# Encoder block with expert retrieval: output products start after 104 of 128 activation blocks instead of 124

## The chip, the cores and the metric

One core of one Trainium2 chip. The metric is the device time of one execution in microseconds (us), median of three runs; less is better.

## The reference

One layer on 512 tokens of width 1024: a mixer (gated convolution and a linear recurrence), then a retrieval over 16384 single-neuron experts, then a norm. The change is in the retrieval:

```python
q = (xb @ w_q).reshape(p, PEER_HEADS, 2, PEER_DK_HALF)
sc = jnp.einsum('phcd,hcnd->phcn', q, sub_keys).astype(jnp.float32)
top_s, top_i = lax.top_k(sc, PEER_TOPK)          # 16 of 128 keys, twice per head
...                                              # 16 of the 256 pairs: best_s, idx
g = jax.nn.softmax(best_s, axis=-1)
act = jax.nn.gelu(jnp.einsum('phkd,pd->phk', expert_u[idx], xb), approximate=False)
coef = (g * act.astype(jnp.float32)).astype(xb.dtype)
return jnp.einsum('phk,phkd->pd', coef, expert_v[idx])   # p = tokens, h = 8, k = 16
```

Each token uses 128 experts (8 heads by 16). All numbers are float32.

## The kernel before

**Two ways to the same sum.** For 384 tokens (three tiles of 128) the kernel is dense: it multiplies them with all 16384 experts, in 128 blocks of 128 experts, and weights the result with a gate matrix that is zero but at the chosen experts. For the other 128 tokens it is sparse: it gathers the 128 chosen rows of `expert_u` and `expert_v` per token. 64 of the dense tokens take their first product (with `expert_u`) from the sparse way too, so a dense activation block is 128 experts by 320 tokens.

**Jobs.** The dense work is a list of 256 jobs, one block of weights (512 KB) each. A u job loads a block of `uT`, multiplies it with the tokens (24 matmuls of 320 columns, `u_chunk`) and puts GELU of the result in an `act` tile, two blocks to a tile. A v job multiplies block n's gated activations with its block of `expert_v` into six accumulators (18 matmuls of 512 columns, L1037). Float32 weights are split into a high part `whi` (ScalarE, ACT, L78) and a low part `wlo` (VectorE, DVE, L83), and each product is three matmuls. Weights are loaded five jobs ahead (`w_load(k + 5)`), `whi` is made three ahead, `wlo` two ahead.

**Order.** `CE` u jobs come first, then v jobs and the remaining u jobs alternate, then v jobs alone. With CE = 124 that is u0 to u123, four pairs (v, u), then v4 to v127; the last three v jobs are done in a tail. The `act` ring holds 32 blocks (RB). Older blocks go to memory: one store of two blocks (`Ad<-act`, L845), one reload before use (`act<-Ad`, L911). v jobs run in the order `vorder`, which begins at block `v0`; blocks from v0 on need no store.

**What else runs in the u part.** DVE also does the top-16 searches, the gate steps and the dots of the sparse way. A gate step builds one-hot matrices for eight tokens (L627, L632; ACT L643), PE multiplies them, ACT copies the result into `stg` (L667, two buffers), and SP stores it to `Gd` (L678; the last store stands on ACT's queue). The last 16 gate steps (four tokens each, in f32: L617, L620, matmuls L655) wait until the dots of the 64 tokens are done. At u job KD = CE - 6 every gate step must be done; at job CE - 5 the first gates are read back (`gt<-Gd`, L898). A planner `turn()` hands out DVE's time: after each job it emits searches, gate steps or dots until DVE's planned time catches up with PE's, at most two dots a job, no dot in the last QU = 6 jobs before CE, and dots only up to DR times the jobs since they began.

**Sparse steps.** One dot is a gather of 128 rows by GpSimd (POOL, `rows<-in_u_dram`, L767, 512 KB) and one DVE instruction (`scr`, L788) with its accumulator read. There are 64 + 128 dots, then 128 sums (`ys`, L804, rows of `expert_v`). Whatever the u part left over is emitted in the v part: after v job n until the count reaches `share`, rising linearly from v3 on, less 0.31 per job once blocks are reloaded.

**Gates in the v part.** v job n takes its gates from a tile that was read from `Gd`: 16 blocks at a time, in three loads of 1024 KB (L885), alternately into the memory of `h2` (free once the last u job is done) and into `gt`; the first 16 blocks come as two times eight (three loads of 512 KB each, L898). `v_gated` makes `cf` (ACT L918, DVE L920) and `ch` (ACT L924), `v_rest` makes `cl` (DVE L931), for two blocks at a time.

All of this is recorded with a manual schedule: within an engine, and within each DMA queue (SP's, POOL's), instructions run in the order in which they are emitted.

Of the kernel before, what the change touches and what calls it, by code (L numbers as in the profile page):

```python
# [8 lines left out]
F32 = mybir.dt.float32  # L9
# [12 lines left out]
NE = 128  # L22
# [12 lines left out]
def block_kernel(ctx, tc, xT, small, w_ada1, w_ada, b_ada, w_in, w_r, w_i, w_out, w_q, keys, uT, u, v, final_g, out):  # L35
# [4 lines left out]
    persist = ctx.enter_context(tc.tile_pool(name="persist", bufs=1))  # L40
# [27 lines left out]
    h2 = persist.tile([128, 2, KB, T], FR, name="h2")  # L68
# [434 lines left out]
    NG = (T - 128) // 16  # L503
# [309 lines left out]
    ld = lambda k: h2l[:, k, T - NU:]  # L813
    jobs = [("u", c) for c in range(CE)]
    for n in range(NE):
        jobs.append(("v", n))
        if CE + n < NE:
            jobs.append(("u", CE + n))
    wraw, whi, wlo = {}, {}, {}
    v0 = max(CE - RB + 3, 0) // 8 * 8 + 8  # L820
    vorder = list(range(v0, NE)) + list(range(v0))

    def w_load(k):
        if k < len(jobs):
            kind, i = jobs[k]
            wraw[k] = load_w(uT[i] if kind == "u" else
                             v[vorder[i] * 128:(vorder[i] + 1) * 128, :].rearrange("p (k e) -> p k e", k=KB))

    def w_high(k):
        if k < len(jobs):  # L830
            whi[k] = high(wraw[k])

    def w_low(k):
        if k < len(jobs):
            wlo[k] = low(wraw.pop(k), whi[k])
# [14 lines left out]
    def u_evict():  # L850
        if unread:
            c, ps = unread.pop()
            if c % 2 == 0:
                act[c // 2] = ring.tile([128, 2, NU], F32, name="act", bufs=RB // 2)
            nc.scalar.activation(act[c // 2][:, c % 2], ps, AF.Gelu)  # L855

    def u_chunk(k, pool):
        c = jobs[k][1]
        ps = pool.tile([128, NU], F32, name="ps_act", bufs=2)
        mm3(ps, whi.pop(k), wlo.pop(k), hd, ld, range(KB), True, True)  # L860
        u_evict()
        unread.append((c, ps))
        q = c // 2 - RB // 2 + 2
        if c % 2 == 0 and 0 <= q < v0 // 2:
            spill(q)
        pe[0] += 3530
        dve[0] += 1140
        ac[0] += 1400

    gbuf, g16, gdone = {}, {}, set()  # L870
    coef = {}

    def load_g16(m, t):
        if m not in g16:
            if m % 32:
                big = g16[16] if m > 16 else persist.tile([128, 32, 16, 16], F32, name="h2")[:, 0:NG]
            else:
                big = gt8.rearrange("p s g i t -> p (s g i t)").rearrange("p (g i t) -> p g i t", i=16, t=16)
            g16[m] = big
            for k in range(0, 16, 2):  # L880
                gbuf[m + k] = big[:, :, k:k + 2, :]
        for k in range(0, 16, 8):
            cc = vorder[m + k]
            if k == 0 and vorder[m + 8] == cc + 8:
                nc.sync.dma_start(g16[m][:, 8 * t - 8:8 * t], Gd[t][:, :, cc:cc + 16, :].rearrange("g j i t -> j g i t"))  # L885
                return
            nc.sync.dma_start(g16[m][:, 8 * t - 8:8 * t, k:k + 8],
                              Gd[t][:, :, cc:cc + 8, :].rearrange("g j i t -> j g i t"))

    def v_gates(n):  # L890
        if n >= NE or n in gdone:
            return
        gdone.add(n)
        cc = vorder[n]
        if n < 16 and n % 8 == 0:
            gt = gt8[:, n // 8]
            for t in (2, 3, 1):
                nc.sync.dma_start(gt[:, 8 * t - 8:8 * t], Gd[t][:, :, cc:cc + 8, :].rearrange("g j i t -> j g i t"))  # L898
            for k in range(0, 8, 2):
                gbuf[n + k] = gt[:, :, k:k + 2, :]  # L900
        for t in range(1, NT):
            m = n + (4 - t if n < 16 else 13 - 3 * t)
            if m >= 16 and m % 16 == 0 and m < NE:
                load_g16(m, t)

    def v_act(q):
        if q < NE // 2:
            c = vorder[2 * q] // 2
            if act[c] is None:
                act[c] = ring.tile([128, 2, NU], F32, name="act", bufs=RB // 2)  # L910
                nc.sync.dma_start(act[c].rearrange("p c t -> p (c t)"), Ad[c])  # L911

    def v_gated(q):
        if q < NE // 2:
            cf = vp.tile([128, 2, ND], F32, name="cf", bufs=1)
            g = gbuf.pop(2 * q)
            nb = XB // 16
            nc.scalar.activation(cf[:, :, 0:XB].rearrange("p c (g t) -> p c g t", t=16),  # L918
                                 g[:, 0:nb].rearrange("p g c t -> p c g t"), AF.Copy)
            nc.vector.tensor_mul(cf[:, :, XB:].rearrange("p c (g t) -> p c g t", t=16),  # L920
                                 act.pop(vorder[2 * q] // 2).rearrange("p c (g t) -> p c g t", t=16),
                                 g[:, nb:].rearrange("p g c t -> p c g t"))
            ch = vp.tile([128, 2, ND], FR, name="ch", bufs=2)
            nc.scalar.activation(ch, cf, AF.Copy)  # L924
            coef[q] = (cf, ch)

    def v_rest(q):
        if q < NE // 2:
            cf, ch = coef[q]
            cl = vp.tile([128, 2, ND], FR, name="cl", bufs=2)  # L930
            nc.vector.tensor_sub(cl, cf, ch.bitcast(F32))  # L931
            coef[q] = (ch, cl)
# [6 lines left out]
    given = {"s": 0, "r": 0, "g": 0, "d": 0}  # L939
    KD = CE - XE - 1  # L940
    first = []

    def turn(k):

        awake = [g for g in "gsrd" if g in gens and asleep[g] <= k]
        if "d" in awake and (given["d"] >= DR * (k + 1 - first[0]) or k >= CE - QU or xd > k % 2):
            awake.remove("d")
# [22 lines left out]
    for k in range(CE):  # L970
# [12 lines left out]
        while dve[0] < RHO * pe[0] or k == KD:  # L983
# [7 lines left out]
            n = next(gens[g], 0)  # L991
# [13 lines left out]
        if k == KD:  # L1005
# [4 lines left out]
            gt8 = vp.tile([128, 2, NG, 8, 16], F32, name="gt", bufs=1)  # L1010
        m = k - CE + XE
        if 0 <= m < XE:
            for n in [0] if m < 2 else range(5) if m == XE - 1 else [8]:
                v_gates(n)
# [17 lines left out]
    def v_chunk(n, b):  # L1032
        hi, lo, ch, cl = vsp[n]
        bs = slice(b * 128, (b + 1) * 128)
        for st, mv, first, last in ((ch, hi, n == 0, False), (ch, lo, False, False), (cl, hi, False, n == NE - 1)):
            for e in range(2):
                nc.tensor.matmul(accs[b][e], st[:, bs], mv[:, e * 512:(e + 1) * 512], start=first, stop=last)  # L1037
# [12 lines left out]
        nc.vector.tensor_add(frow[0], frow[0], frow[1])  # L1050

    sparse = chain(dot_gen, sum_gen)
    steps, done = len(usteps) - len(bdone) + 128, 0
    for k in range(CE, len(jobs)):
        w_load(k + 5)
        w_high(k + 3)
        w_low(k + 2)
        kind, n = jobs[k]
        if kind == "u":
            u_chunk(k, psP)  # L1060
        else:
            q, e = divmod(n, 2)
            v_gates(n + 5)
            if e == 0:
                v_act(q + 4)
                v_gated(q + 1)
            else:
                v_rest(q + 1)
            vsp[n] = [w.pop(k).rearrange("p k e -> p (k e)") for w in (whi, wlo)] + [c[:, e] for c in coef[q]]
            if n < NE - VT:  # L1070
                for b in range(3):
                    v_chunk(n, b)
                del vsp[n]
            u_evict()
            pe[0] += 4090
            dve[0] += 2005
        if kind == "v":
            share = min(max(n + 1 - QV, 0) / (NE - VE - QV), 1) * (steps + 0.31 * (NE - RB)) - 0.31 * max(n + 1 - RB, 0)
            while done < share and next(sparse, None):
                done += 1  # L1080
    fin = vp.tile([128, 2, 3, D], F32, name="gt", bufs=1)
# [47 lines left out]
VE = 1  # L1129
# [2 lines left out]
NS = 56000  # L1132
DS = 1.0
XD = 2
CE = 124
GB_E = 5
DR = 1.1
QU = 6
QV = 3
RB = 32  # L1140
# [54 lines left out]
```

## Time and profile before

| | us |
|---|---|
| median of 3 runs (1408.8 to 1412.49) | 1411.27 |
| profiled execution, time | 1413.22 |
| its span, first to last instruction | 1411.5 |
| u part, before the first v job (309.30 to 832.15) | 522.85 |
| v0 to the start of the tail (832.15 to 1378.72) | 546.57 |
| tail (1378.72 to the end) | 32.78 |

PE (matmuls) is busy 95% of the span, DVE 87%, ACT 49%, POOL 38%. In the rows that the prediction shows, PEclk is the granted clock of PE as a share of full speed, and the DMA share is the mean busy share of 16 DMA engines. Overlapping packets take it a little over 1. A window's row gives busy time and number of instructions of each engine in turn.

### The profile page before, as it was taken

To read this page: it belongs to the slowest core of one execution; us is meant where nothing else is said; L and a number is where in the kernel's file an instruction comes from. 1 tells how busy PE (TensorE), PEld (TensorE's weight loads), DVE (VectorE), ACT (ScalarE), POOL (GpSimd) and SP (SyncE) were. 2 spreads that over 40 slices of the span, in tenths; PEclk is the share of its full clock that TensorE was granted. 3 is DMA by queue.
4 is the path that set the end of the run, shared out by engine and by line. 5 is a ranking of instruction groups with operands and counts; after the bars stand their busy time and mean duration, and the time that the engine had idled before them with its cause. 6 is when DMAs were issued, how large, how long until landed. Compare 5 with 4: busy or idle time off the path is not lost.

```text
span 1411.5 us, 21746 instructions
## 1 busy us (share of the span) xinstructions
PE 1336.9 (95%) x7739; PEld 1144.7 (81%) x7739; DVE 1222.1 (87%) x2332; ACT 687.6 (49%) x1178; POOL 538.0 (38%) x334
## 2 busy tenths in 40 slices
PE   5999998999998999999999999899989999999995
PEld 2666787779998999998989998777778888878884
DVE  6766555899998999999989847799989889898998
ACT  4544433545377697797744444233333434343442
POOL 0000000000233145344545404576666667576760
PEclk9999999999999999999999999999999999999998
DMA  9675322124678899999999997999999999999994
GB/s 378 225 265 181 124 90 97 61 83 134 203 253 300 290 344 397 357 355 355 417 382 388 403 314 244 411 378 410 403 415 411 404 404 416 412 405 410 406 382 165
DMA packets 146929, 440.07 MB, mean 312 GB/s; under 512 B 14722, under 2 KB 42370, under 8 KB 144772
## 3 DMA queue, kind: packets, MB, share of 16 engines
q1 hardware_dynamic: 99812, 267.75, 51.5%
q0 software_dynamic: 46720, 169.89, 30.8%
q8 instruction: 60, 0.98, 0.3%
q10 hardware_dynamic: 288, 1.05, 0.2%
q14 instruction: 49, 0.40, 0.1%
HBM read 393.54 MB, written 45.09 MB: 311 GB/s over the span
## 4 chain that ended last, share of the span: by engine, by line
DVE 27%; PE 23%; DMA 16%; issue 13%; ACT 4%; DVEq 0%; SPq 0%; ACTq 0%
DMA wraw<-in_v_dram 13%; DVE wlo L83 5%; PE ps_act L92 5%; PE ps_act L94 5%; PE ps_act L93 5%; PE acc L1037 5%; DVE scr L788 4%; DVE ys L804 4%; DMA Gd<-stg 2%; DVE cf L920 2%; DVE cl L931 2%; DVE oh L627 2%; ACT whi L78 1%; DVE rep L457 1%; PE ps_gt L658 1%
## 5 line engine op out<-in xcount | busy, mean ns | idle before, releaser
L78 ACT ACTIVATE whi<-wraw 128x1024 fp32r<-128x1024 f32 x292 | 308.7, 1057 | 404.1 <-DMA wraw<-in_v_dram 157.7
L83 DVE TENSOR_TENSOR wlo<-wraw,whi 128x1024 fp32r<-128x1024 f32 x292 | 356.1, 1220 | 112.5 <-ACT whi L78 111.3
L92 PE MATMUL ps_act<-h,whi 128*128 128x320 f32 x1024 | 322.5, 315 | 8.1 <-ACT act L855 6.9
L94 PE MATMUL ps_act<-h,wlo 128*128 128x320 f32 x1024 | 317.1, 310 | 0.6 <-DVE wlo L83 0.6
L93 PE MATMUL ps_act<-h,whi 128*128 128x320 f32 x1024 | 317.1, 310 | 0.0
L767 POOL DMA_INDIRECT rows<-in_u_dram,idx_s x128 | 201.3, 1573 | 189.0 <-DVE scr L788 162.4
L767 POOL DMA_INDIRECT rows<-in_v_dram,idx_s x128 | 222.7, 1740 | 108.7 <-DVE ys L804 84.9
L1037 PE MATMUL acc<-whi,ch 128*128 128x512 f32 x750 | 233.7, 393 | 9.5 <-ACT ch L924 9.2
L1037 PE MATMUL acc<-whi,cl 128*128 128x512 f32 x750 | 234.6, 394 | 6.1 <-DVE cl L931 6.1
L1037 PE MATMUL acc<-wlo,ch 128*128 128x512 f32 x750 | 233.6, 393 | 0.0
L767 POOL DMA_INDIRECT rows<-in_u_dram,idx_b x64 | 108.9, 1701 | 255.7 <-DVE scr L788 171.8
L92 PEld LDWEIGHTS ps_act<-h,whi 128*128 128x128 f32 x1024 | 193.2, 189 | 10.8 <-ACT act L855 8.7
L94 PEld LDWEIGHTS ps_act<-h,wlo 128*128 128x128 f32 x1024 | 192.9, 188 | 0.9 <-DVE wlo L83 0.9
L93 PEld LDWEIGHTS ps_act<-h,whi 128*128 128x128 f32 x1024 | 193.3, 189 | 0.2
L1037 PEld LDWEIGHTS acc<-whi,ch 128*128 128x128 f32 x750 | 141.6, 189 | 40.7 <-ACT ch L924 10.9
L1037 PEld LDWEIGHTS acc<-whi,cl 128*128 128x128 f32 x750 | 141.6, 190 | 40.1 <-DVE cl L931 11.1
L1037 PEld LDWEIGHTS acc<-wlo,ch 128*128 128x128 f32 x750 | 142.1, 189 | 29.9
L804 DVE SCALAR_TENSOR_TENSOR ys<-rows,acts,ys 128x1024 f32<-128x1024 f32 x127 | 162.6, 1281 | 1.7
L788 DVE SCALAR_TENSOR_TENSOR scr<-rows,h2n 128x1024 f16<-128x1024 f32 x128 | 156.2, 1220 | 2.3 <-DMA rows<-in_u_dram,idx_s 0.6
L643 ACT ACTIVATE igh<-oh,gl 128x128 f16<-128x128 f16 x320 | 104.0, 432 | 47.8 <-DVE oh L627 47.6
L408 POOL DMA_DIRECT2D x1d<-xn x8 | 4.6, 569 | 281.7 <-DVE wlo L83 234.6
L92 PE MATMUL ps_z<-h,whi 128*128 128x512 f32 x224 | 90.8, 409 | 3.2 <-ACT h L216 2.9
(260 smaller groups left out, 1691.2 us busy)
## 6 DMA issues: line engine op xcount, KB each, us to landing
wraw<-in_uT_dram SPq DMA_DIRECT2D x128, 512.0 KB, 6.8
wraw<-in_v_dram SPq DMA_DIRECT2D x128, 512.0 KB, 9.3
Gd<-stg SPq DMA_DIRECT2D x46, 512.0 KB, 9.2
wada<-in_w_ada_dram SPq DMA_DIRECT2D x16, 1024.0 KB, 5.1
Ad<-act SPq DMA_DIRECT2D x48, 320.0 KB, 7.1
act<-Ad SPq DMA_DIRECT2D x48, 320.0 KB, 12.2
h<-Gd SPq DMA_DIRECT2D x12, 1024.0 KB, 18.3
wraw<-in_w_in_dram SPq DMA_DIRECT2D x20, 512.0 KB, 6.1
```

What stands on the lines that cost most here:

```text
L78: nc.scalar.activation(hi, raw, AF.Copy)
L83: nc.vector.tensor_sub(lo, raw, hi.bitcast(F32))
L92: nc.tensor.matmul(ps, hi[:, k, :], xh(k), start=first and k == ks[0], stop=False)
L93: nc.tensor.matmul(ps, hi[:, k, :], xl(k), start=False, stop=False)
L94: nc.tensor.matmul(ps, lo[:, k, :], xh(k), start=False, stop=last and k == ks[-1])
L627: nc.vector.tensor_tensor(flat.rearrange("p (q n b) -> p q n b", q=8, b=2), io2[:, None, :, :].to_broadcast(shp), sij[:, a0].rearrange("p ...
L643: nc.scalar.activation(ig[:, 1, k // 2, :, k % 2], of[:, k // 2, 0, :, k % 2], AF.Copy, scale=gl[:, t0 + k:t0 + k + 1])
L767: nc.gpsimd.indirect_dma_start(out=r[:, :], out_offset=None, in_=table, in_offset=bass.IndirectOffsetOnAxis(ap=idxs[:, k:k + 1], axis=0))
L788: nc.vector.scalar_tensor_tensor(scr, rows.pop(n), 1.0, hn, op0=OP.mult, op1=OP.mult, accum_out=dst[:, k:k + 1])
L804: nc.vector.scalar_tensor_tensor(ys, rows.pop(k), acts[:, k:k + 1], ys, op0=OP.mult, op1=OP.add)
L920: nc.vector.tensor_mul(cf[:, :, XB:].rearrange("p c (g t) -> p c g t", t=16), act.pop(vorder[2 * q] // 2).rearrange("p c (g t) -> p c g t" ...
L1037: nc.tensor.matmul(accs[b][e], st[:, bs], mv[:, e * 512:(e + 1) * 512], start=first, stop=last)
```

## The change

```diff
     def load_g16(m, t):
         if m not in g16:
-            if m % 32:
-                big = g16[16] if m > 16 else persist.tile([128, 32, 16, 16], F32, name="h2")[:, 0:NG]
+            if m % 32 == 0:
+                big = g16[32] if m > 32 else persist.tile([128, 32, 16, 16], F32, name="h2")[:, 0:NG]
...
     def v_gates(n):
...
-        if n < 16 and n % 8 == 0:
-            gt = gt8[:, n // 8]
+        if n < 32 and n % 8 == 0:
+            gt = gt8[:, n // 8 % 2]
...
-            m = n + (4 - t if n < 16 else 13 - 3 * t)
-            if m >= 16 and m % 16 == 0 and m < NE:
+            m = n + (4 - t if n < 32 else 13 - 3 * t)
+            if m >= 32 and m % 16 == 0 and m < NE:
                 load_g16(m, t)
...
+    room = [MX if n < NE - CE else 1.62 if n < 32 else 1.5 for n in range(NE)]
...
-            share = min(max(n + 1 - QV, 0) / (NE - VE - QV), 1) * (steps + 0.31 * (NE - RB)) - 0.31 * max(n + 1 - RB, 0)
+            share = steps * sum(room[QV:n + 1]) / sum(room[QV:NE - VE])
...
-CE = 124
+CE = 104
+MX = 3.4
-DR = 1.1
+DR = 0.9
```

In the program it builds: u0 to u103, 24 pairs (v0, u104) to (v23, u127), then v24 to v127. `v0` moves from block 96 to block 80, so 40 act tiles are stored and reloaded instead of 48. The gates of the first 32 blocks come eight at a time, and the 16-block loads begin with block 32 of the order. The first v job finds 72 dots done instead of 112. The number of dots, sums, gate steps and matmuls is the same.

DVE between early v jobs (numbers behind the names tell the buffers apart). Before, at v6 and v7, with no u job between them:

```order
L83 TENSOR_TENSOR wlo_9701<-wraw_9594,whi_9665 128x1024
L920 TENSOR_TENSOR cf_9703<-act_8590,gt_9187 128x2x320
L788 SCALAR_TENSOR_TENSOR scr_9728,acts_2625<-rows_9659,h2n_1878 128x1024
L788 SCALAR_TENSOR_TENSOR scr_9732,acts_2625<-rows_9689,h2n_1878 128x1024
L83 TENSOR_TENSOR wlo_9738<-wraw_9625,whi_9699 128x1024
L931 TENSOR_TENSOR cl_9740<-cf_9703,ch_9706 128x768
L788 SCALAR_TENSOR_TENSOR scr_9762,acts_2625<-rows_9693,h2n_1878 128x1024
L788 SCALAR_TENSOR_TENSOR scr_9766,acts_2625<-rows_9726,h2n_1878 128x1024
```

After, at u111, v8 and the start of u112 (a `wlo` is for the job two further on):

```order
L83 TENSOR_TENSOR wlo_9092<-wraw_8967,whi_9042 128x1024
L83 TENSOR_TENSOR wlo_9123<-wraw_9009,whi_9090 128x1024
L920 TENSOR_TENSOR cf_9125<-act_7949,gt_8367 128x2x320
L788 SCALAR_TENSOR_TENSOR scr_9151,acts_2625<-rows_9072,h2n_1878 128x1024
L788 SCALAR_TENSOR_TENSOR scr_9155,acts_2625<-rows2_9076,h2n_1878 128x1024
L788 SCALAR_TENSOR_TENSOR scr_9159,acts_2625<-rows_9080,h2n_1878 128x1024
L788 SCALAR_TENSOR_TENSOR scr_9163,acts_2625<-rows_9082,h2n_1878 128x1024
L83 TENSOR_TENSOR wlo_9169<-wraw_9040,whi_9121 128x1024
```

Where each v job had two dots, a pair of jobs now has four (three in every fourth pair), all behind the v job's `wlo`.

DVE at the last gate steps, `selB` being the selected keys of the 64 tokens. Before, at u102 and the start of u103:

```order
L83 TENSOR_TENSOR wlo_8412<-wraw_8276,whi_8408 128x1024
L788 SCALAR_TENSOR_TENSOR scr_8443,acts_2625<-rows_8348,h2n_1878 128x1024
L617 TENSOR_TENSOR oh8_8445<-iota_76,selB_2624 128x512
L620 TENSOR_SCALAR oh8_8445<-iota_76,selB_2624 128x128 x4
L617 TENSOR_TENSOR oh8_8457<-iota_76,selB_2624 128x512
L620 TENSOR_SCALAR oh8_8457<-iota_76,selB_2624 128x128 x4
L83 TENSOR_TENSOR wlo_8473<-wraw_8317,whi_8469 128x1024
L788 SCALAR_TENSOR_TENSOR scr_8504,acts_2625<-rows_8400,h2n_1878 128x1024
```

After, at u91 and the start of u92:

```order
L83 TENSOR_TENSOR wlo_7922<-wraw_7725,whi_7918 128x1024
L617 TENSOR_TENSOR oh8_7951<-iota_76,selB_2624 128x512
L620 TENSOR_SCALAR oh8_7951<-iota_76,selB_2624 128x128 x4
L617 TENSOR_TENSOR oh8_7963<-iota_76,selB_2624 128x512
L620 TENSOR_SCALAR oh8_7963<-iota_76,selB_2624 128x128 x4
L617 TENSOR_TENSOR oh8_7978<-iota_76,selB_2624 128x512
L620 TENSOR_SCALAR oh8_7978<-iota_76,selB_2624 128x128 x4
L83 TENSOR_TENSOR wlo_7994<-wraw_7762,whi_7990 128x1024
```

The 16 steps stood in u94 to u111, one or two a job with dots between; now they stand in u90 to u94, five in the first job and two or three in each other one, with one dot among them.

SP's queue at the first gate loads into `h2`. Before (v8 to v10, ten weight loads after the last load for a u job):

```order
L73 DMA wraw<-in_uT_dram 128x1024
L73 DMA wraw<-in_v_dram 128x1024 x10
L885 DMA h_9774<-Gd_2596 128x8x256
L73 DMA wraw<-in_v_dram 128x1024
L885 DMA h_9774<-Gd_2597 128x8x256
```

After (v24 to v26):

```order
L73 DMA wraw<-in_uT_dram 128x1024
L73 DMA wraw<-in_v_dram 128x1024 x6
L885 DMA h_10333<-Gd_2596 128x8x256
L73 DMA wraw<-in_v_dram 128x1024
L885 DMA h_10333<-Gd_2597 128x8x256
```

The three loads into `h2` stand one job behind the last u job (v24, right after u127), where four v jobs lay between; the loads of eight blocks for v16 and v24 stand further ahead, at v11 and v19, inside the pairs.

## Prediction

> **What bounds the kernel now.** First the page's head, then a table of windows by stage, then in the worst stage the chain and the waits.
>
> ```profile
> span 1411.5 us, 21746 instructions
> PE 1336.9 (95%) x7739; PEld 1144.7 (81%) x7739; DVE 1222.1 (87%) x2332; ACT 687.6 (49%) x1178; POOL 538.0 (38%) x334
> ...
> 379.39:666.81 287.42, 275.69 (x2153) 269.38 (x2152) 278.73 (x583) 222.18 (x492) 110.82 (x64) 0.99 0.91 325
> 666.81:832.15 165.34, 160.71 (x1173) 159.32 (x1171) 141.05 (x231) 85.80 (x162) 72.28 (x49) 0.99 1.02 392
> 832.15:863.21 31.06, 30.77 (x171) 27.55 (x170) 15.63 (x18) 11.98 (x16) 2.74 (x2) 1.00 0.64 218
> 863.21:1062.72 199.51, 187.36 (x794) 150.93 (x793) 180.54 (x248) 69.69 (x90) 132.38 (x82) 0.97 1.01 394
> 1062.72:1378.72 316.00, 312.83 (x1369) 257.67 (x1368) 295.86 (x274) 120.36 (x153) 207.72 (x120) 0.99 1.03 405
> ```
>
> The columns are PE, PEld, DVE, ACT, POOL, clock, DMA share, GB/s. The u part to 666.81 is DVE's: 278.73 of 287.42 us. Then DVE has spare time and DMA is full. 832.15 to 863.21 holds the four pairs, with DVE at half and DMA at 218 GB/s. From 863.21 on PE, DVE and DMA are all nearly full.
>
> What a job costs PE undisturbed (window's length, busy PE, matmuls):
>
> ```profile
> 796.95:828.63 31.68, 31.68 (x218) 1.00 1.04 383
> 1046.40:1168.80 122.40, 122.40 (x541) 1.00 1.03 407
> ```
>
> Nine u jobs (24 matmuls each) in 31.68 is 3.52 us. Thirty v jobs (18 each) in 122.40 is 4.08. So the three v windows hold 4 u + 4 v = 30.4, 44 v = 179.5 and 76 v = 310.1 us of PE, and lose 0.7, 20.0 and 5.9: 26.6 us. That is the most that this part can give. Where the 20 go:
>
> ```profile
> 884.49 21.70 DMA wraw<-in_v_dram
> ...
> ACT whi L78 <- DMA wraw<-in_v_dram: 69.7, 19, 9.6
> ...
> 908.46 0.77 PE L1037 MATMUL acc<-whi,ch 128*128 128x512 f32 x2 [4.27 <-ACT ch L924]
> ...
> 909.87 1.06 PE L1037 MATMUL acc<-whi,cl 128*128 128x512 f32 x2
> 910.73 1.06 PE L1037 MATMUL acc<-whi,ch 128*128 128x512 f32 x2
> ...
> 914.74 0.62 PE L1037 MATMUL acc<-wlo,ch 128*128 128x512 f32 x2
> 915.20 0.61 PE L1037 MATMUL acc<-whi,cl 128*128 128x512 f32 x2
> ```
>
> One weight load took 21.70 us, ACT waited for such loads 19 times, PE stood 4.27 us, and its pairs of matmuls then came 0.86 us apart instead of 0.46. That was at v13, after the three 1024 KB loads into `h2` at v8 to v10.
>
> **The change, part by part.** Prices of DVE are start to start, from the timeline, and from the groups:
>
> ```profile
> 727.35 1.23 DVE L788 SCALAR_TENSOR_TENSOR scr<-rows,h2n 128x1024 f16<-128x1024 f32 x1
> ...
> 728.50 1.22 DVE L83 TENSOR_TENSOR wlo<-wraw,whi 128x1024 fp32r<-128x1024 f32 x1
> 729.63 1.22 DVE L788 SCALAR_TENSOR_TENSOR scr<-rows,h2n 128x1024 f16<-128x1024 f32 x1
> ...
> 730.78 0.68 DVE L617 TENSOR_TENSOR oh<-iota,selB 128x512 f32<-128x512 f32 x1
> ...
> 732.41 0.68 DVE L617 TENSOR_TENSOR oh<-iota,selB 128x512 f32<-128x512 f32 x1
> ...
> L931 DVE TENSOR_TENSOR cl<-cf,ch 128x768 fp32r<-128x768 f32 x64 | 60.8, 951 | 0.0
> L920 DVE TENSOR_TENSOR cf<-act,gt 128x640 f32<-128x640 f32 x32 | 26.2, 818 | 0.0
> L627 DVE TENSOR_TENSOR oh<-io,selT 128x2048 f16<-128x2048 f16 x40 | 48.7, 1218 | 0.0
> L632 DVE TENSOR_TENSOR igh<-oh,gh 128x1024 f16<-128x1024 f16 x40 | 27.7, 692 | 1.4
> ```
>
> `wlo` 1.13; a dot 1.15 and the accumulator's read behind it, taken as 1.26; a last gate step (730.78 to 732.41) 1.63; an eight-token gate step 1.9; `cf` and `cl` together 1.77 for two v jobs, 0.8 a job since starts overlap by a tenth.
>
> *1. u part, 20 jobs shorter.* DVE was busy 278.73 + 141.05 = 419.8 us from 379.39 to 832.15. Away go 20 `wlo` (22.6) and 40 dots (72 instead of 112 before the first v job: 50.4): 346.8 stay. DVE's idle time comes on top. The 3% of the first window go with the DVE-bound stretch, some 300 us: 9. In u86 to u89 there is one dot a job (2.4 us against 3.52), and the last gate steps then wait for PE's product of the 64 tokens: 4.5. In u98 to u103 DVE has `wlo` and one `cf` and `cl`, 8.6 against 21.1: 12.5. From u64 to u83 the planner catches up on dots: 30 dots, 20 `wlo` and 13 gate steps are 85 us of DVE, while 20 weights, 30 gathers, 13 times 0.524 MB of gates and ten `act` stores are 36.3 MB, 90 us at the 405 GB/s above; rows gathered ahead carry part of it: 2 (bounds 0 and 5). The crowded last gate steps wait for their stores:
>
> ```profile
> ACT stg L667 <- DMA Gd<-stg: 8.8, 2, 7.4
> ...
> DMA to landing us min/median/max: 6.3/9.2/15.2
> ...
> 688.00 15.62 DMA Gd<-stg
> 703.64 15.71 DMA Gd<-stg
> ```
>
> A group of four steps is 6.5 us of DVE and 1.4 of `wlo`, 7.9. A `stg` buffer is filled and landed in 7.9 + 9.2, so two buffers give 8.6 a group: 3 us over four groups, and something for the first, whose buffer is stored only as the steps begin. I take 4 (bounds 0 and 8.8, the row's whole wait). ACT does 40 eight-token steps in fewer jobs and was already busy 222.18 of 287.42: 3 more (0 to 8). Sum: 346.8 + 9 + 4.5 + 12.5 + 2 + 4 + 3 = 381.8, so v0 at 761.2. Before, less 20 jobs of 3.52, it would be 761.75: a gain of 0.5, bounds -10 and +10. The dots that left the u part cost it nothing more; step 2 has them.
>
> *2. The pairs.* v0 to v2 with their u jobs have no dots: 22.8 + 0.7 as before. In the other 21 pairs (PE 159.6) stand 79 dots (99.5), 42 `wlo` (47.5) and `cf`, `cl` at 0.8 (16.8): DVE 163.8. DMA moves, by
>
> ```profile
> wraw<-in_v_dram SPq DMA_DIRECT2D x128, 512.0 KB, 9.3
> Ad<-act SPq DMA_DIRECT2D x48, 320.0 KB, 7.1
> act<-Ad SPq DMA_DIRECT2D x48, 320.0 KB, 12.2
> h<-Gd SPq DMA_DIRECT2D x12, 1024.0 KB, 18.3
> gt<-Gd SPq DMA_DIRECT2D x6, 512.0 KB, 10.0
> rows<-in_u_dram,idx_s POOLq DMA_INDIRECT x128, 8.5
> ```
>
> 42 weight blocks, 79 gathers (128 rows of 4 KB, also 512 KB) and six half gate loads: 127 x 0.524 = 66.6 MB, at the 405 GB/s of the last window 164.4 us. So three engines agree on 160 to 164; I take 164.3. The smaller gate loads: 10.0 us for 512 KB against 18.3 for 1024, no dearer than 10% for 3.1 MB, so 0 to 0.8 us; 0 taken, under DVE's cover. The Trainium skill (DMA: Bandwidth & Descriptors, Rules for kernel authors) asks for 1 MiB or more per DMA, which speaks against this part; by its table, 341 GB/s at 1 MB, an estimate of 300 at half of that would add 1.2 us. The weight loads here, 512 KB each, run in a stream of 405, so I do not follow it.
>
> *3. v24 to v47.* 24 x 4.08 = 97.9. Now 41 dots and sums stand there instead of two a job: DVE 41 x 1.26 + 24 x 1.93 = 98.0. DMA: 24 weights, 41 gathers, six gate loads of 1.05 MB, four reloads: 41.7 MB, at 405 GB/s 103.0. The loads into `h2` come three in 12 us again, so something like v13 returns, but with 1.7 gathers a job and not 2. I add 5: 102.9 (bounds 97.9 and, stretched like the second v window, 108.8). SP comes to the first of them while u127 still runs and waits for its last matmul, at most a u job, with the weights of v30 behind it; these have six v jobs, 24 us, and land in 9.3: 0.
>
> *4. v48 on.* 76 jobs at 1.5 steps instead of 1.6, eight fewer reloads; 310.1 + 3 (0 to 5.9). The eight stores of 320 KB (2.6 MB, 6.5 us of DMA at 405) were in the u part; they free DMA time, no PE time.
>
> *5. Tail.* One sum more in the last six jobs: +1.2.
>
> v0 to the tail: 23.5 + 164.3 + 102.9 + 313.1 = 603.8. Before, with 20 u jobs more, 546.57 + 70.4 = 617.0: 13.2 less. Sum: -0.5 - 13.2 + 1.2 = -12.5 against the profiled execution (1413.22, of which 1.7 lies outside the span): 1400.7. The median of the runs is 1.95 lower, so 1398.8: I say 1399.
>
> **The rivals.**
>
> *A, no change: DMA takes it back.* Steps 2 and 3 need 108.3 MB. At the 394 GB/s that the stalled window got, that is 275 us instead of 267.2. With late weights in the last 76 jobs as before (+2.9) the time is 1399 + 10.7, 1410. For it: the DMA share is 1.01 even where PE loses 20 us, and gathers come in fours. Against: the next window moves 405 with hardly a loss. By the Trainium skill's limit of 358 GB/s per core (DMA: Bandwidth & Descriptors, Where 436 GB/s comes from) it would be 302 us; the 405 above disagree, and I give that no chance of its own.
>
> *B, slower: the gate stores.* The crowded steps put eight stores (four groups of two halves) into five jobs, and the first gate loads, in memory that `stg` may share, come two jobs behind the last. If a store lands in the row's maximum, 15.2, each group takes (7.9 + 15.2) / 2 = 11.6 instead of 8.6: +12; the last store, 6 us later, then holds `gt<-Gd`, behind it the weights on SP's queue and `cf` on ACT: +6. Time 1399 + 18 = 1417. It takes the gain away from some 13 us to landing. Before, the chain twice had 15.6 us there. Against: dots, the other load, pause in these jobs.
>
> *C, more gain.* The u part gains 10, v24 on loses nothing: 1399 - 9.5 - 5 - 3 = 1381.5. For it: the demand of v48 on falls from 1.6 to 1.5 gathers a job. Against: DVE at 163.8 in the pairs leaves no room to catch up.
>
> **How the numbers follow.** My sum 0.57, A 0.2, B 0.1, C 0.13. Within 0.3% of 1411.27 is 1407 to 1415.5, about what three runs (1408.8 to 1412.49) can tell. Faster: my sum nearly whole (0.55), C, and a little of A (0.04): 0.72. Same: most of A and a little of the sum, 0.17. Slower: B and a remainder, 0.11. The range, 1385 to 1412, holds all of A and half of C and leaves out B; the forecast's own is 1390 to 1406.
>
> **What would show it.** v0 begins near 761 (over 770: B, and `stg` waits for `Gd<-stg` over 15 us). Pairs from v3 on take 7.7 to 7.9 us, DVE over 95% there; 8.2 or more is A. PE's loss from v24 to v47 is some 5 us, after it 3. ACT's wait for `wraw<-in_v_dram` falls well under the 69.7 us of this stage. I would be wrong if the pairs starve for rows.

## The result: 0.9% slower, and the profile after

| | before | after |
|---|---|---|
| median, four runs each (us) | 1410.84 (1408.80 to 1412.49) | 1423.51 (1419.97 to 1425.53) |
| profiled execution, time / span | 1413.22 / 1411.5 | 1425.53 / 1423.8 |
| after by before, 95% interval | | 1.0088 (1.0064 to 1.0112) |

The forecast was 1399, and 1385 to 1412. The time lies outside, on the other side of no change. First the head of the page after, then its windows by stage: v0 to v2, v3 to v23, a stall within that, v24 to v47, v48 to v123 (columns as before).

```profile
span 1423.8 us, 21746 instructions
PE 1342.6 (94%) x7739; PEld 1144.6 (80%) x7739; DVE 1224.1 (86%) x2332; ACT 685.5 (48%) x1178; POOL 523.5 (37%) x334
```

```profile
763.37:787.36 23.99, 23.22 (x126) 20.78 (x127) 12.49 (x13) 10.32 (x14) 0.00 (x0) 1.00 0.84 273
787.36:961.86 174.50, 166.14 (x885) 146.93 (x883) 153.60 (x214) 61.28 (x84) 108.70 (x77) 0.97 0.96 364
930.00:953.90 23.90, 17.87 (x84) 14.71 (x84) 14.50 (x21) 6.06 (x9) 9.21 (x8) 0.86 0.85 312
961.86:1070.10 108.24, 101.51 (x434) 82.04 (x433) 96.99 (x132) 37.78 (x49) 69.55 (x42) 0.97 1.02 393
1070.10:1390.35 320.25, 314.16 (x1370) 257.27 (x1368) 301.58 (x283) 119.85 (x153) 211.64 (x124) 0.99 1.03 407
```

The u part ends as forecast, at 763.4. The pairs v3 to v23 take 174.5 us, not 164.3. They run at PE's own pace, but for two places: u117 and v14, and u125, v22 and u126 (the third row: granted clock 0.86, DMA at 312 GB/s, DVE busy 14.50 of 23.90). Around the second place the timeline shows SP's queue and PE (start, duration, what; in brackets the idle time before it):

```profile
918.36 0.33 SPq L73 DMA_DIRECT2D wraw<-in_uT_dram  x1
918.73 10.06 SPq L898 DMA_DIRECT2D gt<-Gd  x3
928.89 3.05 SPq L73 DMA_DIRECT2D wraw<-in_v_dram  x1
...
942.36 1.22 PE L1037 MATMUL acc<-whi,ch 128*128 128x512 f32 x2 [4.76 <-ACT whi L78]
```

The three gate loads at v19 hold SP's queue for 10.06 us; the weight block behind them, which otherwise follows at once, is issued from 928.89 on. The chain of waits passes through it, and then ACT:

```profile
928.30 0.59 DVE scr L788
928.89 12.28 DMA wraw<-in_v_dram
941.25 1.06 ACT whi L78
```

So the weight lands 22.4 us after its turn, and PE stands 4.76 us. Over the whole third row PE is idle for 6.03 us, and the granted clock is 0.86. Since in DVE's order the dots stand behind `wlo`, the gathers stop too, and DMA, at 407 GB/s up to then, falls to 211 GB/s from 942.36 to 953.90, in the middle of a stage that it limits:

```profile
945.85 1.80 POOL L767 DMA_INDIRECT rows<-in_u_dram,idx_s  x1 [11.83 <-DVE scr L788]
```

The place at v14 has the same pattern. In this stage ACT waited for weights (total, times, longest):

```profile
ACT whi L78 <- DMA wraw<-in_v_dram: 31.0, 6, 12.6
...
ACT whi L78 <- DMA wraw<-in_uT_dram: 18.9, 8, 5.6
```

The trace of before already held the issue time, in rows that the prediction did not read: its three loads for v0 and for v8, the same half-megabyte loads, each time kept SP's queue for 6 to 8 us.

```profile
811.10 8.37 SPq L898 DMA_DIRECT2D gt<-Gd  x3
...
821.95 6.45 SPq L898 DMA_DIRECT2D gt<-Gd  x3
```

There it cost PE nothing: the prediction's row 796.95:828.63 has PE busy throughout. From 811 to 822 POOL issued one gather, at v19 (918 to 930) six. So these rows show how long the queue is held, not what that costs; that the gathers beside the burst make the difference fits both places, and no run tested it alone.

### The profile page after: what moved, and what is told of

Same layout as the page of the kernel before. It is cut to its first block, busy times and chain, and to the rows that moved or that the text cites. A ratio compares the mean times of both kernels' runs of the same rounds, so it can differ in the third digit from the quotient of the medians.

```text
span 1423.8 us, 21746 instructions
## 1 busy us (share of the span) xinstructions
PE 1342.6 (94%) x7739; PEld 1144.6 (80%) x7739; DVE 1224.1 (86%) x2332; ACT 685.5 (48%) x1178; POOL 523.5 (37%) x334
## 3 DMA queue, kind: packets, MB, share of 16 engines
q10 hardware_dynamic: 288, 1.05, 0.2%
## 4 chain that ended last, share of the span: by engine, by line
issue 35%; DVE 20%; DMA 16%; POOL 8%; PE 3%; ACT 1%; DVEq 0%; POOLq 0%; SPq 0%; ACTq 0%
DMA wraw<-in_v_dram 12%; POOL rows L767 8%; DVE wlo L83 4%; DVE ys L804 3%; DVE scr L788 3%; PE acc L1037 2%; DVE cl L931 2%; DVE cf L920 2%; DMA rows<-in_u_dram,idx_s 2%; DVE rep L457 1%; DVE ti L462 1%; DVE ti L455 1%; ACT whi L78 1%; DMA act<-Ad 1%; DVE top L460 1%
## 5 line engine op out<-in xcount | busy, mean ns | idle before, releaser
L94 PE MATMUL ps_act<-h,wlo 128*128 128x320 f32 x1024 | 318.2, 311 | 2.2 <-DVE wlo L83 2.0
L767 POOL DMA_INDIRECT rows<-in_u_dram,idx_s x128 | 190.9, 1492 | 196.5 <-DVE scr L788 170.8
L767 POOL DMA_INDIRECT rows<-in_v_dram,idx_s x128 | 218.4, 1706 | 108.8 <-DVE ys L804 88.8
L92 PEld LDWEIGHTS ps_act<-h,whi 128*128 128x128 f32 x1024 | 193.5, 189 | 13.7 <-ACT act L855 10.6
## 6 DMA issues: line engine op xcount, KB each, us to landing
act<-Ad SPq DMA_DIRECT2D x40, 320.0 KB, 10.9
```

The source lines that it names most:

```text
L92: nc.tensor.matmul(ps, hi[:, k, :], xh(k), start=first and k == ks[0], stop=False)
L94: nc.tensor.matmul(ps, lo[:, k, :], xh(k), start=False, stop=last and k == ks[-1])
L767: nc.gpsimd.indirect_dma_start(out=r[:, :], out_offset=None, in_=table, in_offset=bass.IndirectOffsetOnAxis(ap=idxs[:, k:k + 1], axis=0))
```

## Experiments

Times are medians, ratios are to the kernel before in the same runs, with 95% intervals; before lay at 1410.5 to 1411.9. Stage times are from each kernel's profile; v3 to v23 holds 21 pairs for CE 104, 13 pairs and eight v jobs for CE 112, and one pair and 20 v jobs for CE 124.

| kernel | CE | time (range) | ratio | v3-23 | v24-47 | v48-123 |
|---|---|---|---|---|---|---|
| before | 124 | 1411 | 1 | 96.7 | 110.4 | 316.0 |
| after | 104 | 1423.5 (1420.0-1425.5) | 1.0088 (1.0064-1.0112) | 174.5 | 108.2 | 320.3 |
| e1_no_early | 104 | 1408.5 (1405.3-1412.1) | 0.9984 (0.9967-1.0000) | 160.0 | 104.4 | 319.5 |
| e2_spread | 104 | 1411.2 (1408.7-1413.7) | 0.9998 (0.9985-1.0011) | 160.8 | 108.2 | 319.7 |
| e3_actq | 104 | 1415.0 (1411.9-1416.9) | 1.0027 (1.0016-1.0039) | 160.0 | 106.5 | 322.8 |
| e4_layout | 104 | 1419.6 (1414.6-1423.6) | 1.0073 (1.0047-1.0100) | 160.0 | 104.1 | 318.2 |
| e11_burst_act | 104 | 1421.0 (1419.2-1422.2) | 1.0068 (1.0051-1.0085) | 170.3 | 105.1 | 323.3 |
| e5_qv0 | 104 | 1403.3 (1400.8-1406.2) | 0.9933 (0.9911-0.9955) | 165.6 | 104.0 | 314.8 |
| e6_h2late | 104 | 1410.1 (1407.3-1415.4) | 0.9988 (0.9973-1.0003) | 160.0 | 107.9 | 319.0 |
| e8_both | 104 | 1403.6 (1396.5-1406.2) | 0.9931 (0.9900-0.9961) | 162.7 | 106.3 | 314.2 |
| e10_mx24 | 104 | 1418.7 (1417.9-1419.3) | 1.0048 (1.0032-1.0065) | 160.0 | 103.3 | 331.6 |
| e7_before_spread | 124 | 1409.1 (1406.2-1412.3) | 0.9972 (0.9955-0.9989) | 95.8 | 105.1 | 316.5 |
| e9_before_qv0 | 124 | 1395.2 (1394.7-1396.5) | 0.9885 (0.9869-0.9902) | 89.7 | 103.3 | 313.8 |
| e16_before_qv0_2 (e9 again) | 124 | 1396.1 (1394.4-1397.7) | 0.9893 (0.9865-0.9921) | 89.9 | 103.8 | 313.9 |
| e12_ce112 | 112 | 1403.0 (1400.3-1406.9) | 0.9943 (0.9926-0.9961) | 132.7 | 107.9 | 317.0 |
| e13_no_early_qv0 | 104 | 1397.6 (1396.6-1400.8) | 0.9907 (0.9877-0.9937) | 160.0 | 103.4 | 314.4 |
| e14_before_eights | 124 | 1399.2 (1398.2-1401.5) | 0.9920 (0.9892-0.9948) | 94.9 | 100.1 | 313.5 |
| e15_before_room | 124 | 1392.6 (1391.0-1393.7) | 0.9866 (0.9838-0.9893) | 90.9 | 100.4 | 311.5 |

### The loads in the pairs

**e1_no_early**, the loads left out:

```diff
         if n < 32 and n % 8 == 0:
...
-            for t in (2, 3, 1):
+            for t in (2, 3, 1) if n < 16 else ():
```

> This kernel leaves out the six loads of gates for v16 to v31 (v jobs there use the gates of v0 to v15 again), nothing else. Theory T (gate loads in 512-byte packets, three at once, hold up SP's queue and the weights behind them): the two stalls in the pairs go, 4.4 us at v14 and 8.8 at v19 to v21; v3 to v23 takes 160 to 165 us instead of 174.5, and the time is 1410 to 1413. Rival R1 (bytes: 3.1 MB less at 405 GB/s): 7.8 us less, 1416, spread over all pairs. Rival R2 (four dots a pair are too many for DVE and the gathers): the stalls stay, 1421 to 1424.

1408.5, some 15 us less than after, more than either theory gave. The stage (v3 to v23) is PE's 159.6 with 0.4 over it:

```profile
787.19:947.21 160.02, 160.02 (x885) 144.78 (x883) 157.12 (x220) 61.98 (x84) 113.88 (x80) 1.00 1.00 387
```

R2, too many dots, falls: the row holds more of them than after's, 80 gathers against 77. R1 falls as well: 3.1 MB are 7.8 us, and 14.5 went.

**e2_spread**, the same loads one at a time:

```diff
+    EARLY = {6: (16, 2), 8: (16, 3), 10: (16, 1), 13: (24, 2), 15: (24, 3), 17: (24, 1)}   # v job: (first block, tile)
...
+            v_early(n)
             v_gates(n + 5)
```

> The same six loads, each alone at its own v job: for v16 at v6, v8, v10 instead of three at v11, for v24 at v13, v15, v17 instead of three at v19. T with the burst as the cause: a single load of 512 KB is small against the five weights that are loaded ahead; most of the 13.2 us goes, 1411 to 1416. T with the packets as the cause, however they are spaced: each load still holds the weights up, by a third of a stall, under the five weights ahead or not: 1416 to 1421. R1 and R2: as the changed kernel, 1422 to 1425.

1411.2: 12.3 us less than after with the same bytes in the same packets, the burst theory's number. The stage's window, and one of the loads on SP's queue with the weight behind it:

```profile
786.90:947.74 160.84, 160.28 (x884) 144.79 (x883) 153.97 (x214) 61.63 (x84) 106.19 (x78) 1.00 1.01 395
```

```profile
866.46 0.43 SPq L912 DMA_DIRECT2D gt<-Gd  x1
867.22 0.79 SPq L73 DMA_DIRECT2D wraw<-in_v_dram  x1
```

A load alone takes 0.43 us to issue, three in a row took 10.06. It is the succession that costs here. The kernel now equals the one before; the rest of the forecast gain is still missing.

**e4_layout**, bursts kept, longer runs:

```diff
-    Gd = {t: dram.tile([8, 128, 128, 16], F32, name=f"Gd{t}") for t in range(1, NT)}
+    Gd = {t: dram.tile([128, 16, 8, 128], F32, name=f"Gd{t}") for t in range(1, NT)}
...
```

> Places, queue and bytes of all loads as in the changed kernel, but Gd is laid out in blocks of eight columns, so that every gate load reads and writes runs of 4 KB a partition (512 B and 1 KB now), and the stores in the u part write runs of 512 B (4 KB now). T with small packets as the cause: the v part (v0 to the tail) falls from 627 us to 603 to 612, with gate loads landing in 6 to 9 us; the u part grows by 0 to 10. Time 1402 to 1416. R1 (bytes) and T with the burst or the queue's order alone, whatever the packets: v part 622 to 628, time 1423 to 1434.

The v part is 607.9 us, as this theory wanted, and v0 begins 8.1 us later (771.44), within the 10 allowed; the median, 1419.6, is above the range, its profiled run (1414.6) in it. The burst at v19 and the pairs' window:

```profile
920.67 1.38 SPq L896 DMA_DIRECT2D gt<-Gd  x3
```

```profile
797.05:957.08 160.03, 160.03 (x885) 144.79 (x884) 154.35 (x214) 61.73 (x84) 109.33 (x78) 1.00 1.00 399
957.08:1061.13 104.05, 99.45 (x434) 80.63 (x433) 97.80 (x134) 37.87 (x49) 69.69 (x43) 1.00 1.02 406
```

Three loads of the same size at the same places, in 4 KB runs, hold the queue 1.38 us and cost PE nothing. So a burst hurts by its many small packets: three times 1024 of 512 B in after, three times 128 of 4 KB here. As the bytes are the same, number and size of the packets are not told apart.

**e11_burst_act** and **e3_actq**, another queue:

```diff
 e11: the changed kernel
-                nc.sync.dma_start(gt[:, 8 * t - 8:8 * t], ...
+                (nc.sync if n < 16 else nc.scalar).dma_start(gt[:, 8 * t - 8:8 * t], ...
 e3: e2_spread, all gate loads from v6 on
-            nc.sync.dma_start(gt8[...  and  nc.sync.dma_start(g16[m][...
+            nc.scalar.dma_start(gt8[...  and  nc.scalar.dma_start(g16[m][...
```

> The changed kernel with its six early loads where they were, three at v11 and three at v19, but issued on ACT's queue. If the burst hurts because weights stand behind it on SP's queue: v3 to v23 falls from 174.5 us to 160 to 164, time 1409 to 1413. If it hurts because of what small packets take from the engines, whatever the queue: the pairs stay above 168 us, or ACT waits for the late gates at v14 and v22; time 1417 to 1425.

> As e2_spread, with all gate loads from v6 on (512 KB and 1 MB) issued on ACT's queue, so that no weight stands behind one. T with the queue's order as the cause: weights land within 12 us, the losses after v24 (10 us) and after v48 (10 us) shrink too: 1400 to 1410. If packets of the three queues take turns and that alone is the cost: gates land late (over 25 us), ACT waits for them before its copy and weights get a third of the turns: 1416 to 1430. R1: as e2_spread, within 2 us.

1421.0 is the second expectation for e11; 1415.0 lies in no range given for e3, just under its second. The way was one that neither had. On ACT's queue, ACT itself stands while its loads are issued (e11 at v11, then e3's third load into `h2`, at v26):

```profile
846.33 12.99 ACTq L898 DMA_DIRECT2D gt<-Gd  x3
859.36 0.44 ACT L855 ACTIVATE act<-ps_act 128x320 f32<-128x320 f32 x1 [11.98 <-issue]
```

```profile
961.45 9.78 ACTq L885 DMA_DIRECT2D h<-Gd  x1
971.27 0.31 ACT L927 ACTIVATE cf<-gt 128x128 f32<-128x128 f32 x1 [8.78 <-issue]
```

GELU and `whi` wait behind it. The burst is not cured by another queue; the engine that issues it pays.

### After v24: spacing or bytes

**e5_qv0** (on e2_spread) lets the sparse steps begin at v0, **e10_mx24** (on e5) puts fewer of them into the pairs, **e6_h2late** (on e2) spaces the loads after v24, **e8_both** joins e5 and e6.

```diff
 e5
-QV = 3
+QV = 0
 e10, besides
-MX = 3.4
+MX = 2.4
 e6 (first block 48: a third of a 16-block load into h2)
+             21: (32, 2), 23: (32, 3), 25: (32, 1), 30: (40, 2), 33: (40, 3), 36: (40, 1),
+             28: (48, 2), 35: (48, 3), 39: (48, 1)}
...
-        if n < 32 and n % 8 == 0:
+        if n < 48 and n % 8 == 0:
```

> As e2_spread, with dots from v0 on (QV 0, not 3): some 11 dots fall into v0 to v2, where DMA moved 330 GB/s and less, and the steps after v32 become 1.57 a job instead of 1.64. Theory D (from v24 on the time is the bytes: 1.64 gathers a job, weights, reloads and gates ask for some 427 GB/s where 412 are to be had): five gathers, 2.7 MB, fewer from v48 on are 6.6 us less there (319.7 to 313 to 315) and 1 to 2 us less before; time 1402 to 1406. Rival G (the losses after v24 come from the gate loads, whatever the gathers): v48 on stays at 318 to 320, time 1410 to 1413.

> As e5_qv0, with MX 2.4 instead of 3.4: 2.8 dots a pair (3.56 there), 1.75 steps a job after v32 (1.57 there). D (from v24 on every gather is paid in bytes, 1.28 us each): the pairs fall from 165.6 to 160 (PE's own), v48 on grows from 314.8 by some 12 gathers, 12 to 16 us; time 1411 to 1417. If bytes are not the limit of v48 on: 1398 to 1404.

> As e2_spread, with the gates of v32 to v47 also eight at a time (one load each at v21, v23, v25 and v30, v33, v36), and the first three loads of 1 MB into h2, for v48, at v28, v35 and v39 instead of for v32 at v24, v25, v26. Bytes are the same. Theory B (the burst of three): v24 to v47 falls from 108.2 us to 99 to 102, time 1402 to 1406. Theory D (the bytes alone): what v29 gains is lost again by v47: v24 to v47 stays at 106 to 109, time 1409 to 1412.

> e5_qv0 and e6_h2late together. If B and D both hold, each in its stage: v24 to v47 at 98 to 101, v48 on at 313 to 315, time 1394 to 1400. If only one holds: 1402 to 1406. If neither: 1409 to 1413.

v48 to v123 in e2, e5 and e10 (the last bracket before the clock is the number of gathers):

```profile
1055.94:1375.61 319.67, 312.75 (x1370) 255.97 (x1368) 301.39 (x282) 120.12 (x153) 223.20 (x124) 1.00 1.03 407
```

```profile
1055.25:1370.08 314.83, 311.82 (x1370) 256.21 (x1369) 296.53 (x275) 119.53 (x152) 202.65 (x118) 1.00 1.03 406
```

```profile
1048.94:1380.58 331.64, 319.77 (x1369) 259.51 (x1368) 310.94 (x298) 119.51 (x153) 230.71 (x133) 0.98 1.03 406
```

118, 124 and 133 gathers take 314.8, 319.7 and 331.6 us, always at 406 to 407 GB/s: 15 gathers more are 16.8 us, 1.1 each, against 1.29 for 0.524 MB at 406. So G falls, and bytes fit as the limit (D). DVE, busy 94% in all three rows, would fit nearly as well at some 1.26 us a step; but of its 20.7 us idle in e10, 18.7 are waits for `whi`, and ACT makes `whi` late because it waits for weights:

```profile
ACT whi L78 <- DMA wraw<-in_v_dram: 114.8, 41, 8.2
...
DVE wlo L83 <- ACT whi L78: 18.7, 8, 4.7
```

From v24 to v47 e6 does not decide. Its time is what D expected: v24 to v31 took 34.3 us instead of 39.3, v32 to v47 73.5 instead of 69.0; 0.4 us is left. But its new stall, at v39 and v40, has a wait that its own edit brings, and that e2 does not have in this stage: the gates of v40, whose last load stands at v36, landed late, while the DMA share was 1.05:

```profile
1016.69 0.82 DVE L934 TENSOR_TENSOR cf<-act,gt 128x640 f32<-128x640 f32 x1 [7.87 <-DMA gt<-Gd]
```

So theory B, right in the pairs, is neither shown nor refuted here. e8 lies in the range for one theory alone, and has the same late gates (6.9 us). (e10 is 1.7 us above its range; its pairs fell to 160.0 as expected.)

### The same edits in the kernel before

**e7_before_spread** and **e9_before_qv0** (CE 124):

```diff
 e7
+            if n in (5, 8, 10):
+                load_g16(16, {5: 2, 8: 3, 10: 1}[n])
             v_gates(n + 5)
 e9, besides
-QV = 3
+QV = 0
```

> The kernel before, CE 124, with its three loads of 1 MB for v16 at v5, v8, v10 instead of v8, v9, v10. B: the stall at v13 and v14 (6.2 us) goes, or most of it: 1404 to 1408. D: v4 to v23 is short of bytes (394 GB/s got), the stall comes elsewhere: 1409 to 1412.

> The kernel before, CE 124, with the two edits that helped the changed one: its three loads of 1 MB spread (v5, v8, v10) and sparse steps from v0 on (QV 0, not 3). Theory W (the early v jobs themselves are a wash: what the u part saves the v part pays in bytes): 3.2 gathers fewer after v48, some 4 us, time 1403 to 1406, the same as the changed kernel with both edits (1403.3). Rival E (early v jobs gain once the burst is gone): 1408 to 1412, 5 us or more behind it.

> e9_before_qv0 once more, on the chip of the three others: 1394 to 1397.

**e12_ce112** is e5_qv0 with CE = 112.

> As e5_qv0 with CE 112 (81 dots done before v0, 16 pairs), between 104 and 124. W: the same within the noise, 1402 to 1407. E, if early v jobs gain by their number: half-way, 1405 to 1409, with the kernel before with both edits at 1409 or more.

Spacing alone gave 2.8 us: the stall moved from v13 to v16 (D). With dots from v0 on the kernel before reaches 1395.2, and 1396.1 again, below every theory of mine. Its v0 to v2, v3 to v23, v24 to v47 and v48 to v123:

```profile
831.18:854.61 23.43, 23.14 (x128) 20.66 (x127) 16.97 (x23) 9.54 (x13) 8.20 (x6) 1.00 0.89 331
854.61:944.31 89.70, 89.64 (x404) 74.35 (x403) 84.15 (x117) 33.19 (x44) 62.32 (x39) 1.00 1.00 390
944.31:1047.65 103.34, 100.09 (x433) 80.53 (x432) 95.15 (x127) 38.99 (x50) 66.40 (x42) 1.00 1.03 415
1047.65:1361.48 313.83, 312.53 (x1370) 256.23 (x1368) 297.12 (x275) 119.93 (x152) 204.43 (x118) 1.00 1.03 409
```

v4 to v47, which lost 20.0 us before (199.5 against 179.5), now lose 5.9. Six gathers in v0 to v2, where DMA had moved 214 GB/s, and three loads 12 and 7 us apart did what 20 moved blocks were to do. With both edits in each, CE 104 is slower than CE 124, by 8 us in the medians and by 6 to 7 in the ratios to before, and CE 112 lies with CE 104: W and E both fall.

### What the remaining 6 to 8 us are

**e13_no_early_qv0** takes the six loads out of e5 as e1 did; **e14_before_eights** puts such loads into e9; **e15_before_room** gives e9 the changed kernel's way of sharing:

```diff
 e14, on e9
-        if n < 16 and n % 8 == 0:
+        if n < 32 and n % 8 == 0:
...
+            v_early(n)
 e15, on e9
+    room = [3.6 if n < NE - CE else 1.62 if n < 32 else 1.5 for n in range(NE)]
...
+            share = steps * sum(room[QV:n + 1]) / sum(room[QV:NE - VE])
```

> As e5_qv0 (CE 104, sparse steps from v0), but the six loads of gates for v16 to v31 are left out (those v jobs use the gates of v0 to v15 again). Theory P (the 7.7 us by which its v part, less 20 u jobs, stays behind that of e9_before_qv0 are the packets of 512 bytes): v3 to v23 falls from 165.6 to 160, v24 to v47 from 104 to 100 to 102; time 1393 to 1397. Theory M (bytes moved from the u part, where DMA had room, to the v part, where it is the limit): 3.1 MB less at 405 GB/s is at most 7.8 us, and what comes off shows evenly: 1396 to 1400.

> As e9_before_qv0 (CE 124), but the gates of v16 to v31 come eight blocks at a time in six loads of 512-byte packets at v6 to v17, and the first loads of 1 MB, for v32, at v17, v20, v23. Bytes are the same as in e9_before_qv0. P: the small packets cost here too, 4 to 8 us: 1399 to 1404. M: nothing, 1394 to 1397.

> As e9_before_qv0 (CE 124), with the changed kernel's way of sharing: 3.7 steps a pair in v0 to v3 (1.87 before), 1.67 a job to v31, 1.54 after it. Some seven gathers move into the first pairs, where DMA moved 340 GB/s. M: 1.28 us each, less what PE's own pace takes back: 5 to 7 us, 1388 to 1391. If the pairs' DVE is the limit: 1394 to 1397.

The whole v part of after, e5, e9, e13 and e15:

```profile
763.37:1390.35 626.98, 605.04 (x2809) 507.02 (x2809) 564.67 (x639) 229.23 (x300) 389.88 (x243) 0.98 1.00 388
```

```profile
761.65:1370.08 608.43, 597.58 (x2809) 505.19 (x2810) 566.49 (x640) 229.29 (x300) 388.68 (x243) 0.99 1.02 401
```

```profile
831.18:1361.48 530.30, 525.40 (x2331) 431.76 (x2329) 493.39 (x539) 201.65 (x259) 341.35 (x203) 1.00 1.02 404
```

```profile
762.18:1363.99 601.81, 595.01 (x2808) 503.88 (x2809) 566.34 (x640) 229.44 (x300) 392.59 (x243) 1.00 1.02 400
```

```profile
833.38:1359.66 526.28, 522.02 (x2330) 432.51 (x2329) 492.20 (x539) 201.83 (x259) 342.64 (x203) 1.00 1.03 407
```

Length times rate is 244.0 MB in e5 and 214.2 in e9: 29.8 MB more, which at e9's 404 GB/s are 73.8 us, for 70.4 us of u jobs on PE. That is 3.4 us against the move, from bytes alone, with the u part 0.9 longer. e14, the same bytes as e9, is 3.1 us slower than its repeat e16 (P said 4 to 8, M nothing), though the intervals of the two ratios overlap. e13 saves 5.8 us by the medians, 3.7 by the ratios: its time is in M's range, its pairs fall to 160.0 as P has it, but v24 to v47 stays at 103.4 where P wanted 100 to 102. So both may hold, 3 to 4 us each, and their sum is near the difference; the split is an estimate, and not settled. e15 is the fastest kernel of the study, 1392.6, 1.3% under before: gathers moved into the first pairs win 3.4 us over e16. 5 to 7 were expected, and the time lies between the two ranges.

## Why the prediction was wrong

The sum missed its profiled execution by 24.8 us (1425.5 against 1400.7), by its steps:

- **Step 1, u part: held, +2.2.** v0 at 763.4 instead of 761.2. From 379.39 to v0 DVE was busy 348.6 us, against 346.8 in the sum, and idle 35.4, against 35.0 for the six other terms together; the terms were not measured one by one. The wait of `stg` for its stores was 10.9 us in all, 2.1 more than before:

```profile
ACT stg L667 <- DMA Gd<-stg: 10.9, 5, 5.9
```

- **Step 2, pairs: failed, +10.2 (+0.5 in v0 to v2).** The step "smaller gate loads ... 0 taken, under DVE's cover" cost 13.7 us in the stage and 12.3 in the time (e2). It priced the loads by landing time and by bytes. Their price was in the issue: three in a row hold SP's queue, and the weights stand behind them. Which weights stand behind a load, the prediction asked for the loads into `h2` and not for these six. DVE gave no cover, as its dots stand behind `wlo`; it was busy 88% of the stage, not over 95%. The rest was a little too dear: without the burst 160.8 instead of 164.3.
- **Step 3, v24 to v47: mis-sized, +5.3.** 42.5 MB came at 393 GB/s, not at 405. The loss stood where the step put it, behind the loads into `h2`: v29 and v30 together took 16.5 us instead of 8.2, 8.3 of the stage's loss of 10.3, where the step added 5. With these loads spaced (e6) it was gone there and came back at v39 and v40, so what sets its size stays open. With 4 KB runs (e4) the rate was 406, so packet size has a part in it; with CE 124 (e9) it was 415.
- **Step 4, v48 on: failed, +7.2.** "1.5 steps instead of 1.6" was misread from the code: `room` holds weights, and `share` scales them to the steps left. 248 steps over weights of 226.9 make 1.093 x 1.5 = 1.64 a job, against 1.61 before. The prediction's own counts say so too: 79 and 41 steps up to v47 leave 128 of the 248 for the 79 jobs from v48 to v126, 1.62 each. The row has 124 gathers, before had 120; the forecast gain of 3 became a loss of 4.3.
- **Step 5, tail:** 33.4 instead of 33.9.

Rival A had the right direction: DMA took the gain back, the v part running at 388 GB/s on the whole. Its price, 394 GB/s in two stages, was too low. The pairs, 8.3 us each, bear its sign (8.2 or more), but not for its reason alone: the loads' issue held the weights up, and after that DMA stood partly idle. B did not come, nor C. Below the steps lies the larger mistake: the 20 us that v4 to v47 lost before were read as room that more PE time would fill. Without any PE time moved, three loads spaced (e7) took 6.2 of them and gathers from v0 on (e9) another 7.9, while the move brings 30 MB with the 70 us of PE that it brings.

The Trainium skill's rule of 1 MiB or more per DMA (DMA: Bandwidth & Descriptors, Rules for kernel authors), which the prediction set aside, spoke against the right part of the change. The trace bears it out only in part: in e4 loads of 512 KB, three in a row, cost the pairs nothing once their runs were 4 KB. What counted here was many small packets issued in a row.

## What to carry to other kernels

Price a moved load by what it does to the queue that issues it: read how long issuing took in the trace, count its packets, and ask what stands behind it and what moves beside it. Where the DMA share is 1.0, a stall that is removed at one place can come back at another (e7, e6); look for the stage in which DMA idles and move transfers there, before moving work. And where numbers in a table are divided by their own sum, work out the rate that results before pricing it.

## What the runs showed of the hardware

- Issuing is not free of what is in flight. One load of 1024 packets (512 B) was issued in 0.43 us (e2); three in a row took 5.31 to 12.99 us over all runs, and three of 128 packets (4 KB) 1.38 to 4.46 (e4). The engine whose queue it is stands meanwhile: ACT 11.98 us in e11.
- Beside gathers, small packets get few of the bytes. In after, from 858 to 860 us, 177 packets of 4 KB of the gathers and 200 of 512 B of SP's queue began: 0.73 MB against 0.10. From 928 to 932 it was 376 against 229: 1.54 MB against 0.12. The weights in the same queue wait with them. The Trainium skill (DMA: Bandwidth & Descriptors, Queues, rings and completion order) says that each DMA engine goes round between its queues at packet granularity; the first counts agree, the second are not one for one, and no run here shows whether a record of the trace is what that section calls a packet.
